# A two-layer diffusion backbone: the feed-forward network's own work is scheduled ahead of the adaLN vectors and state-space tables made beside it

## The chip, the cores and the metric

The kernel runs on one core of one Trainium2 chip. The time is that of one execution on the device, in microseconds (us), and the median of several executions is compared. TensorE (PE in the profile, with PEld for its weight loads) multiplies matrices, VectorE (DVE), ScalarE (ACT) and GpSimd (POOL) work elementwise, SyncE (SP) issues nearly all DMAs.

## What is computed

Two trunk layers of a backbone over 640 tokens (128 of context, 512 latent) of width 1024:

```python
for l in range(DEPTH):                                   # DEPTH = 2
    mod = silu(c) @ w_ada[l] + b_ada[l]                  # adaLN: shifts, scales, gates
    h   = layer_norm(x) * (1 + scale1) + shift1
    z   = h @ w_in[l]                                    # one combined projection
    mix = concat(ssm(z), neighbourhood_attention(z), gqa(z))
    x   = layer_norm(ALPHA * x + gate1 * (mix @ w_out[l]), g1, b1)
    h   = layer_norm(x) * (1 + scale2) + shift2
    u   = silu(gate(h)) * up(h)                          # SwiGLU: w_ffn_in, 2 x 2816 columns
    x   = layer_norm(ALPHA * x + gate2 * (u @ w_ffn_out[l]), g2, b2)
```

The state-space group (ssm) needs tables of powers of the discretised poles, which depend on the weights of its layer alone. All is float32.

## The kernel before

The 640 tokens are five tiles of 128. A float32 matrix product is three products of halves: each operand is split in a high and a low part (`split`, L283 a cast on ACT, L284 a subtraction on POOL or DVE), and `mm3` (L309 to L313) multiplies high by high, low by high and high by low. Tiles `wh`, `wl` hold split weights (from raw `wr`), `hh`, `hl` the split normalised input, `xs` the split output of the network's first half.

The feed-forward network, `ffn` (L1725), runs over 22 blocks f of 128 hidden columns, in six parts (`PARTS`, 4, 4, 4, 3, 4, 3). A block is made by `ffn_in` (L1624): weights loaded, combined and split (`ffn_in_weights`, L1597 the combinations on DVE), seven products of half-size blocks on PE, their sums on DVE (L1647), two Silu on ACT (L1651 to L1660), the gating (L1663, L1665 on DVE) and the split into `xs` (L283, L284). The first `EARLY` = 2 blocks are made by `ffn_in_plain` without the combinations, a generator of two halves. After each part the part's blocks, collected in `gT`, are multiplied with their rows of `w_ffn_out` (`product`, ten to a part: two halves of 512 columns by five tiles): the gate on DVE (L1764) and the running sum on DVE (L1766, L1771; in the last part `residual`, L1303, which sums rows as well). The last part stands in its own branch (L1773 to L1802): per tile two products into PSUM banks `psS` (two buffers of two banks), then the post-LayerNorm (`post_ln`: L1288 and L1298 on DVE, L257 on ACT, the power -1/2 at L230 on POOL), the next layer's normalisation (L273 on ACT), its transposition (L417 on PE), modulation (L423 on DVE, L425 on ACT), the split into `hh` and `hl`, and the first products with the next layer's `w_in`.

Beside this network the kernel makes what the next layer needs, as `ffn_side` (L1822): two generators, of which each block with f >= `SIDE0` = 2 takes one step. One is adaLN (`ada_side`, 12 half vectors: loads into `ev`, matmuls L381, transpositions L386 and L398). The other is `ssm_tables` (in layer 0 only): after its powers, four groups h of a table B (`powtab`: per group four products L615 and two sums L617 on DVE, then matmuls L631 and L635, transpositions L655, copies L639 and L658, two small operations L642 and L644, stores L646, L648 and L659) and four groups of a table C (L615, L617 and the stores L664). Both work in the four buffers `ev`, which the next layer's weight pieces (`begin`, halves split into `ev` and `ys`) use too. What is left of the side work is asked for at the start of the last part, ahead of its products in the program.

The order of the instructions on each engine is made when the program is built: a scheduler takes, of what is ready by its own count, the instruction that stands first in the program. `tc.high_priority(n)` makes what is written inside it stand n instructions earlier for that choice; `PRIO` is 300 (L1459). Before the change it wraps the preparation and the units of neighbourhood attention only. `tc.issue_after(ins)` holds the side step until the instruction `ins` (here the gating of the block) has been placed.

```python
            for f in range(f0, f0 + nf):
                gT.append(next(plain[f]) if f < self.EARLY else self.ffn_in(l, f, H))
                if f >= self.SIDE0:
                    with self.tc.issue_after(self.mark.ins):
                        next(side, None)
```

Of the kernel before, what the change touches and what calls it, by code (L numbers as in the profile page):

```python
# [157 lines left out]
class Build:  # L158
# [1566 lines left out]
    def ffn(self, l, xs, M, H, nxt, ada):  # L1725
        nc, I = self.nc, self.I
        V, S = nc.vector, nc.scalar
        side = self.ffn_side(l, nxt, ada)
        rows = {}

        def row(key, src):
            if key not in rows:
                rows[key] = self.bcast_row(src)
            return rows[key]

        wo = I["w_ffn_out"][l].rearrange("(k p) n -> p k n", p=128)
        f0 = 0
        for key, cd in (("gp", 0), ("gs", 1)):
            row(key, M["gates"][1, cd])
        for part, nf in enumerate(PARTS):  # L1740
            gT = []
            plain = [self.ffn_in_plain(l, f, H) for f in range(f0, min(f0 + nf, self.EARLY))]
            for p in plain:
                next(p)
            for f in range(f0, f0 + nf):
                gT.append(next(plain[f]) if f < self.EARLY else self.ffn_in(l, f, H))
                if f >= self.SIDE0:
                    with self.tc.issue_after(self.mark.ins):
                        next(side, None)
            last = part == len(PARTS) - 1  # L1750

            def weights(n):
                cs = slice(n * 512, (n + 1) * 512)
                return [b for k0 in range(0, nf, 2) for b in self.wload(wo[:, f0 + k0:f0 + min(k0 + 2, nf), cs])]

            def product(n, i, w, ps=None, sums=None):
                cs = slice(n * 512, (n + 1) * 512)
                ps = ps or self.psA()
                for k in range(nf):
                    a = self.cols(i)  # L1760
                    self.mm3(ps, a(gT[k][0]), a(gT[k][1]), *w[k], k == 0, k == nf - 1)
                g = row("gp", M["gates"][1, 0]) if i == 0 else row("gs", M["gates"][1, 1])
                t = ps
                V.tensor_tensor(out=t, in0=ps, in1=g[:, cs], op=ALU.mult)  # L1764
                if part == 0:
                    V.scalar_tensor_tensor(out=xs[i][:, cs], in0=xs[i][:, cs], scalar=ALPHA, in1=t, op0=ALU.mult,  # L1766
                                           op1=ALU.add)
                elif last:
                    self.residual(xs[i][:, cs], t, sums[n])
                else:  # L1770
                    V.tensor_tensor(out=xs[i][:, cs], in0=xs[i][:, cs], in1=t, op=ALU.add)  # L1771

            if last:  # L1773
                if l + 1 < L:
                    self.function(AF.Exp, self.after)
                w = [weights(n) for n in range(2)]
                junk = self.k4(),
                for _ in side:
                    pass
                if l + 1 < L:  # L1780
                    A = nxt["A"] = self.begin(l + 1, nxt["M"], True)
                for m, i in enumerate(self.ORD):
                    if l + 1 < L:
                        two = self.psS()
                        two = two[:, 0], two[:, 1]
                    else:
                        two = [self.psA() if b else self.psS()[:, 0] for b in self.LB[m]]
                    sums = self.columns("fsum")
                    for n in range(2):
                        product(n, i, w[n], two[n], sums)  # L1790
                    out = self.xout[l][i]
                    parts = self.halves(out) if m == NT - 1 and l == L - 1 else None
                    s = self.post_ln(xs[i], row("lg", I["ln2_g"][l]), row("lb", I["ln2_b"][l]), sums, junk,
                                     self.LNF[l][m], parts)
                    if not parts:
                        nc.sync.dma_start(out, xs[i])
                    if l + 1 < L:
                        self.normalise(xs[i], self.halves(xs[i]), self.stats_of(xs[i], s, junk, "lsn"),
                                       self.NORMV[1])
                        for j in self.ORD[max(m - 1, 0):m] + self.ORD[m:] * (m == NT - 1):  # L1800
                            A["tile_in"](j, xs[j])
                            A["tile_pieces"](j)  # L1802
            else:
                for n in range(2):
                    w = weights(n)
                    for i in self.ORD:
                        product(n, i, w)
            f0 += nf

    def ada_side(self, l, M, nxt):  # L1810
# [104 lines left out]
```

## Time and profile before

| | |
|---|---|
| runs | 1800.53 us median of 3 (1794.71 to 1801.53) |
| profiled execution | 1788.01 us, its span 1786.0 us, mean granted clock 0.960 |
| PE busy | 1641.2 us, 92% of the span, 11624 matmuls |
| DVE busy | 1222.5 us, 68% |
| ACT, POOL busy | 827.3 us (46%), 763.5 us (43%) |
| network of layer 0, its parts | 478 to 941 us, PE busy 444.20 of 463 us |
| network of layer 1, its parts | 1337 to 1758 us, PE busy 411.76 of 421 us |
| layer 0's end and layer 1's first products | 941 to 1003 us, PE busy 49.9 of 62 us |

The span runs from the first to the last instruction of the profiled execution. A busy PE is not a PE at its peak, since the clock that it is granted varies; a stretch in which it is idle or granted less is time that other work could give back. Times in a timeline are microseconds from the start of the span.

### The profile page before, as it was taken

To read this page: it belongs to the slowest core of one execution; us is meant where nothing else is said; L and a number is where in the kernel's file an instruction comes from. 1 tells how busy PE (TensorE), PEld (TensorE's weight loads), DVE (VectorE), ACT (ScalarE), POOL (GpSimd) and SP (SyncE) were. 2 spreads that over 40 slices of the span, in tenths; PEclk is the share of its full clock that TensorE was granted. 3 is DMA by queue.
4 is the path that set the end of the run, shared out by engine and by line. 5 is a ranking of instruction groups with operands and counts; after the bars stand their busy time and mean duration, and the time that the engine had idled before them with its cause. 6 is when DMAs were issued, how large, how long until landed. Compare 5 with 4: busy or idle time off the path is not lost. (4 is left out here: it accounts for less than half of the span.)

```text
span 1786.0 us, 31489 instructions
## 1 busy us (share of the span) xinstructions
PE 1641.2 (92%) x11624; PEld 1435.8 (80%) x11624; DVE 1222.5 (68%) x2460; ACT 827.3 (46%) x1800; POOL 763.5 (43%) x651
## 2 busy tenths in 40 slices
PE   5899899898899999999897989998979999999997
PEld 2898677676788888798796978876859899998995
DVE  5765546627678776778877565565487687876777
ACT  5444446657443334243345556665574242433433
POOL 3853203059235343346266232111785254454463
PEclk9999899798999999999999999998989999999999
DMA  9445767446353645232324243463542231222212
GB/s 335 112 126 139 238 194 213 123 158 203 107 172 122 195 127 182 81 121 71 121 85 157 92 129 96 111 187 115 180 148 85 94 107 59 92 74 69 98 62 81
DMA packets 183114, 234.90 MB, mean 132 GB/s; under 512 B 78960, under 2 KB 112048, under 8 KB 182960
## 3 DMA queue, kind: packets, MB, share of 16 engines
q1 hardware_dynamic: 182960, 232.88, 42.3%
q8 instruction: 92, 1.51, 0.3%
q14 instruction: 62, 0.51, 0.1%
HBM read 203.57 MB, written 29.39 MB: 130 GB/s over the span
## 5 line engine op out<-in xcount | busy, mean ns | idle before, releaser
L284 POOL TENSOR_TENSOR wl<-wr,wh 128x512 fp32r<-128x512 f32 x362 | 504.2, 1413 | 522.8 <-ACT wh L283 343.2
L283 ACT CAST wh<-wr 128x512 fp32r<-128x512 f32 x450 | 275.2, 619 | 383.9 <-DVE wr L1597 88.6
L311 PE MATMUL psM<-hh,wh 128*128 128x320 f32 x560 | 180.3, 322 | 2.3 <-DVE ys L1647 1.1
L313 PE MATMUL psM<-hh,wl 128*128 128x320 f32 x560 | 177.9, 318 | 0.0
L312 PE MATMUL psM<-hl,wh 128*128 128x320 f32 x560 | 177.8, 318 | 0.0
L311 PEld LDWEIGHTS psM<-hh,wh 128*128 128x128 f32 x560 | 108.5, 194 | 6.2 <-issue 1.8
L311 PE MATMUL psT<-hh,wh 128*128 128x320 f32 x352 | 109.9, 312 | 0.0
L313 PEld LDWEIGHTS psM<-hh,wl 128*128 128x128 f32 x560 | 108.6, 194 | 1.5 <-issue 1.4
L312 PE MATMUL psT<-hl,wh 128*128 128x320 f32 x352 | 109.2, 310 | 0.0
L313 PE MATMUL psT<-hh,wl 128*128 128x320 f32 x352 | 109.0, 310 | 0.0
L312 PEld LDWEIGHTS psM<-hl,wh 128*128 128x128 f32 x560 | 108.7, 194 | 0.3
L230 POOL TENSOR_TENSOR sm<-sm,mhalf 128x1 f32<-128x1 f32 (+2 forms) x46 | 54.3, 1182 | 92.3 <-DVE sm L260 49.3
L1647 DVE TENSOR_TENSOR ys<-ys,psM 128x320 f32<-128x320 f32 x140 | 65.0, 481 | 33.8 <-PE psM L313 31.9
L1160 DVE TENSOR_REDUCE psS<-psS 128x1 f32<-128x640 f32 x64 | 52.7, 828 | 47.4 <-PE psS L1157 45.6
L1647 DVE TENSOR_TENSOR ys<-ys,psT 128x320 f32<-128x320 f32 x140 | 65.0, 481 | 28.8 <-PE psT L313 27.7
L311 PE MATMUL psT<-b,wh 128*128 128x320 f32 x240 | 76.5, 319 | 8.3 <-DVE ys L1647 7.4
L311 PE MATMUL psM<-b,wh 128*128 128x320 f32 x240 | 76.1, 317 | 5.8 <-DVE ys L1647 5.8
L284 POOL TENSOR_TENSOR wl<-ws,wh 128x512 fp32r<-128x512 f32 x40 | 53.6, 1340 | 64.4 <-ACT wh L283 62.6
L859 PE MATMUL psT<-ident,ys 128*128 128x128 f32 x440 | 73.2, 285 | 5.8 <-DVE hl L284 3.3
L311 PE MATMUL psM<-wh,xs 128*128 128x512 f32 x190 | 74.9, 394 | 3.7 <-DVE k L1771 3.5
L311 PE MATMUL psT<-wh,xs 128*128 128x512 f32 x190 | 75.6, 398 | 2.9 <-DVE k L1771 2.9
L1597 DVE TENSOR_TENSOR ws<-wr,wr 128x512 f32<-128x512 f32 x40 | 37.0, 926 | 58.9 <-DMA wr<-in_w_ffn_in_dram 28.3
(440 smaller groups left out, 4907.9 us busy)
## 6 DMA issues: line engine op xcount, KB each, us to landing
wr<-in_w_ffn_in_dram SPq DMA_DIRECT2D x88, 512.0 KB, 3.7
ev<-in_w_ada_dram SPq DMA_DIRECT2D x112, 256.0 KB, 4.0
wr<-in_w_ffn_out_dram SPq DMA_DIRECT2D x40, 512.0 KB, 3.9
wr<-in_w_out_dram SPq DMA_DIRECT2D x32, 512.0 KB, 3.6
wr<-in_w_in_dram SPq DMA_DIRECT2D x28, 512.0 KB, 4.8
wa<-in_w_ada_dram SPq DMA_DIRECT2D x24, 512.0 KB, 4.7
k<-in_x_dram SPq DMA_DIRECT2D x10, 512.0 KB, 5.6
xs<-zqk SPq DMA_DIRECT2D x32, 160.0 KB, 3.7
```

The costliest lines, as they stand in the source:

```text
L230: self.nc.gpsimd.tensor_tensor(out=o, in0=v, in1=self.mhalf.broadcast_to([128, v.shape[1]]), op=ALU.pow)
L283: nc.scalar.copy(hi, src)
L284: (lo_eng or nc.vector).tensor_tensor(out=lo, in0=src, in1=hi.bitcast(F32), op=ALU.subtract)
L311: nc.tensor.matmul(ps, lhsT=ah, rhs=bh, start=first, stop=False)
L312: nc.tensor.matmul(ps, lhsT=ah, rhs=bl, start=False, stop=False)
L313: nc.tensor.matmul(ps, lhsT=al, rhs=bh, start=False, stop=last)
L859: self.nc.tensor.transpose(pt[:, j * 128:(j + 1) * 128], s, self.ident)
L1160: V.tensor_reduce(out=m, in_=sp[:, :, 0:320], axis=AX.XY, op=ALU.max, negate=True)
L1597: V.tensor_tensor(out=o, in0=x, in1=y, op=op)
L1647: V.tensor_tensor(out=o, in0=x, in1=y, op=ALU.add)
```

## The change

The blocks f of the network (for f below `EARLY`, their second half) and the products of every part but the last are written inside `high_priority(PRIO)`, in both layers. The side steps, the first halves of the plain blocks and the whole last part are not. No instruction is added or taken away.

```diff
             for f in range(f0, f0 + nf):
-                gT.append(next(plain[f]) if f < self.EARLY else self.ffn_in(l, f, H))
+                with self.tc.high_priority(self.PRIO):
+                    gT.append(next(plain[f]) if f < self.EARLY else self.ffn_in(l, f, H))
                 if f >= self.SIDE0:
                     with self.tc.issue_after(self.mark.ins):
                         next(side, None)
...
             else:
-                for n in range(2):
-                    w = weights(n)
-                    for i in self.ORD:
-                        product(n, i, w)
+                with self.tc.high_priority(self.PRIO):
+                    for n in range(2):
+                        w = weights(n)
+                        for i in self.ORD:
+                            product(n, i, w)
             f0 += nf
```

Behind the first line of the diff the numbers of lines grow by one (L1764 becomes L1765), behind the second by two.

The order of DVE in part 4 of layer 0's network before the change: table C (`ev_9409` to `ev_9415` is its group 1) among the sums and gatings of two blocks.

```order
L1647 TENSOR_TENSOR ys_9300<-ys_9300,psM_9389 128x320
L1665 TENSOR_TENSOR ys_9300<-ys_9300,ys_9301 128x320
L615 TENSOR_TENSOR ev_9409<-k_1346_7183,k_1345_7180 128x512
L615 TENSOR_TENSOR ev_9410<-k_1346_7183,k_1345_7180 128x512
L615 TENSOR_TENSOR ev_9414<-k_1346_7183,k_1345_7180 128x512
L615 TENSOR_TENSOR ev_9415<-k_1346_7183,k_1345_7180 128x512
L1647 TENSOR_TENSOR ys_9301<-ys_9301,psT_9374 128x320
L617 TENSOR_TENSOR ev_9409<-ev_9409,ev_9410 128x512
L617 TENSOR_TENSOR ev_9414<-ev_9414,ev_9415 128x512
L1663 TENSOR_TENSOR ys_9300<-ys_9300,ys_9301 128x320
```

After the change no operation of table C stands in any part of the network on DVE.

The order of DVE at the end of layer 0's network before the change, from the last block's gating (L1665) on: `psS_10467` and `psS_10512` are the products of the last part's first two tiles, `k_888` is the first tile's residual.

```order
L1665 TENSOR_TENSOR ys_10266<-ys_10266,ys_10267 128x320
L284 TENSOR_TENSOR xs_10265<-ys_10266,xs_10264 128x320 x2
L1764 TENSOR_TENSOR psS_10467<-psS_10467,k_982_5298 128x512
L1764 TENSOR_TENSOR psS_10512<-psS_10512,k_982_5298 128x512
L1303 SCALAR_TENSOR_TENSOR k_888_4838,sm_10468<-k_888_4838,psS_10467 128x512
L1303 SCALAR_TENSOR_TENSOR k_886_4835,sm_10513<-k_886_4835,psS_10512 128x512
L1764 TENSOR_TENSOR psS_10467<-psS_10467,k_982_5298 128x512
L1303 SCALAR_TENSOR_TENSOR k_888_4838,sm_10468<-k_888_4838,psS_10467 128x512
L252 TENSOR_SCALAR sm_10495<-sm_10468 128x1
L1764 TENSOR_TENSOR psS_10512<-psS_10512,k_982_5298 128x512
L1303 SCALAR_TENSOR_TENSOR k_886_4835,sm_10513<-k_886_4835,psS_10512 128x512
L260 TENSOR_SCALAR sm_10495<-sm_10495 128x1
```

The next row is the first tile's L1288. The same place after the change begins so:

```order
L1665 TENSOR_TENSOR ys_10266<-ys_10266,ys_10267 128x320
L615 TENSOR_TENSOR ev_8758<-k_1346_7183 128x512
L615 TENSOR_TENSOR ev_8759<-k_1346_7183 128x512
L284 TENSOR_TENSOR xs_10265<-ys_10266,xs_10264 128x320 x2
L617 TENSOR_TENSOR ev_8758<-ev_8758,ev_8759 128x512
L615 TENSOR_TENSOR ev_8763<-k_1346_7183 128x512
L615 TENSOR_TENSOR ev_8764<-k_1346_7183 128x512
L642 TENSOR_TENSOR ev_8929<-eye_146,dcol_5859 16x64
L617 TENSOR_TENSOR ev_8763<-ev_8763,ev_8764 128x512
L1765 TENSOR_TENSOR psS_10467<-psS_10467,k_982_5298 128x512
```

and 42 rows further, with the rest of the 20 L615 and 10 L617 of B's last group and of all of C between, comes to the first tile's LayerNorm:

```order
L1765 TENSOR_TENSOR psS_10754<-psS_10754,k_982_5298 128x512
L615 TENSOR_TENSOR ev_9735<-k_1346_7183,k_1345_7180 128x512
L1303 SCALAR_TENSOR_TENSOR k_806_4440,sm_10755<-k_806_4440,psS_10754 128x512
L617 TENSOR_TENSOR ev_9734<-ev_9734,ev_9735 128x512
L252 TENSOR_SCALAR sm_10778<-sm_10755 128x1
L1765 TENSOR_TENSOR psS_10875<-psS_10875,k_982_5298 128x512
L260 TENSOR_SCALAR sm_10495<-sm_10495 128x1
L1288 SCALAR_TENSOR_TENSOR k_888_4838<-k_888_4838,sm_10495,k_1975_10491 128x1024
L1303 SCALAR_TENSOR_TENSOR k_804_4437,sm_10876<-k_804_4437,psS_10875 128x512
L1298 SCALAR_TENSOR_TENSOR k_888_4838,sm_10501<-k_888_4838,sm_10495,k_1976_10493 128x1024
```

The first L1288 stood behind two tiles' products and now stands behind all ten L1765 and the tables.

On POOL, in the same place, the two powers (L230) of the first tile's statistics stood one behind the other before the change:

```order
L284 TENSOR_TENSOR wl_11157<-wr_11154,wh_11156 128x512
L230 TENSOR_TENSOR sm_10495<-sm_10495,mhalf 128x1
L230 TENSOR_TENSOR sm_10504<-sm_10504,mhalf 128x1
L230 TENSOR_TENSOR sm_10536<-sm_10536,mhalf 128x1
L284 TENSOR_TENSOR wl_11161<-wr_11154,wh_11160 128x512
```

and after it they stand among the splits of the next layer's weights:

```order
L284 TENSOR_TENSOR ys_10421<-wr_10423,ev_10417 128x256
L230 TENSOR_TENSOR sm_10495<-sm_10495,mhalf 128x1
L284 TENSOR_TENSOR ys_10421<-wr_10433,ev_10418 128x256 x2
L284 TENSOR_TENSOR ys_10422<-wr_10433,ev_10419 128x256 x2
L284 TENSOR_TENSOR wl_11287<-wr_11284,wh_11286 128x512
L1010 TENSOR_TENSOR ys_11081<-ys_11081,zt_11082 128x640
L284 TENSOR_TENSOR wl_11291<-wr_11284,wh_11290 128x512
L230 TENSOR_TENSOR sm_10504<-sm_10504,mhalf 128x1
```

The casts into `ev_10416` to `ev_10419`, which those splits read, need `ev` buffers that tables still hold, and `wr_11284` is loaded behind table C's last store on SP.

## Rows read from the trace of the kernel before

**Rows 1.** The page: busy time, share and instructions; one costliest group.

```profile
PE 1641.2 (92%) x11624; PEld 1435.8 (80%) x11624; DVE 1222.5 (68%) x2460; ACT 827.3 (46%) x1800; POOL 763.5 (43%) x651
...
L284 POOL TENSOR_TENSOR wl<-wr,wh 128x512 fp32r<-128x512 f32 x362 | 504.2, 1413 | 522.8 <-ACT wh L283 343.2
```

**Rows 2.** Busy time by stretch: both networks, then layer 0's end in two.

```profile
core 0: us, PE busy (x) PEld busy (x) DVE busy (x) ACT busy (x) POOL busy (x), PEclk, DMA share, GB/s
478.00:941.00 463.00, 444.20 (x3050) 396.02 (x3049) 353.78 (x643) 167.06 (x331) 195.40 (x142) 0.99 0.40 124
1337.00:1758.00 421.00, 411.76 (x2427) 383.78 (x2428) 319.40 (x486) 159.27 (x307) 197.56 (x145) 0.99 0.25 81
941.00:973.00 32.00, 24.56 (x102) 18.75 (x101) 25.19 (x60) 18.45 (x38) 23.11 (x26) 0.95 0.46 149
973.00:1003.00 30.00, 25.37 (x195) 24.24 (x195) 24.24 (x56) 22.55 (x45) 10.76 (x9) 0.94 0.35 124
```

**Rows 3.** What PE waited for, 800 to 880 us.

```profile
engine line waited for: us in total, times, longest us
PE psM L311 <- DVE ys L1647: 3.7, 3, 2.6
PE psT L311 <- DVE ys L1647: 2.9, 1, 2.9
```

**Rows 4.** Busy time by stretch, as rows 2, of 10 us each.

```profile
830.00:840.00 10.00, 7.37 (x44) 7.11 (x43) 9.84 (x17) 3.12 (x7) 3.61 (x3) 0.89 0.28 96
840.00:850.00 10.00, 10.00 (x66) 10.00 (x65) 9.74 (x9) 3.40 (x7) 8.06 (x6) 0.94 0.16 53
850.00:860.00 10.00, 7.06 (x38) 6.80 (x37) 9.60 (x16) 4.22 (x9) 6.16 (x5) 0.83 0.37 107
```

**Rows 5.** Groups of instructions, 478 to 941 us: busy, mean ns | idle before.

```profile
L615 DVE TENSOR_TENSOR ev<-k,k 128x512 f32<-128x512 f32 x16 | 18.8, 1231 | 0.0
...
L615 DVE TENSOR_TENSOR ev<-k 128x512 f32<-128x512 f32 x16 | 13.6, 882 | 0.0
...
L617 DVE TENSOR_TENSOR ev<-ev,ev 128x512 f32<-128x512 f32 x16 | 11.7, 743 | 0.0
...
L631 PE MATMUL psS<-k,ev 128*128 128x32 f32 x64 | 9.2, 275 | 0.0
...
L655 PE MATMUL psS<-ident,ev 128*128 128x128 f32 x32 | 4.8, 272 | 0.0
```

**Rows 6.** Timeline of DVE: start, duration, engine, line.

```profile
841.71 6.90 DVE L615 TENSOR_TENSOR ev<-k,k 128x512 f32<-128x512 f32 x4
...
873.87 2.49 DVE L615 TENSOR_TENSOR ev<-k,k 128x512 f32<-128x512 f32 x4
...
877.28 0.68 DVE L617 TENSOR_TENSOR ev<-ev,ev 128x512 f32<-128x512 f32 x1
```

**Rows 7.** Busy time by stretch, as rows 2.

```profile
870.00:880.00 10.00, 10.00 (x54) 8.85 (x53) 9.90 (x20) 3.57 (x7) 0.00 (x0) 1.00 0.73 239
```

**Rows 8.** Timeline of DVE at layer 0's end.

```profile
944.87 1.74 DVE L284 TENSOR_TENSOR xs<-ys,xs 128x320 fp32r<-128x320 f32 x2 [0.83 <-ACT xs L283]
946.53 1.28 DVE L1764 TENSOR_TENSOR psS<-psS,k 128x512 f32<-128x512 f32 x2
947.73 0.67 DVE L1303 SCALAR_TENSOR_TENSOR k<-k,psS 128x512 f32<-128x512 f32 x1
...
954.29 1.64 DVE L1288 SCALAR_TENSOR_TENSOR k<-k,sm,k 128x1024 f32<-128x1024 f32 x1
...
957.62 1.28 DVE L1298 SCALAR_TENSOR_TENSOR k<-k,sm,k 128x1024 f32<-128x1024 f32 x1 [0.96 <-POOL sm L230]
```

**Rows 9.** Timeline of ACT at layer 0's end.

```profile
960.29 1.15 ACT L257 ACTIVATE k<-k,sm 128x1024 f32<-128x1024 f32 x1 [6.50 <-DVE sm L254]
...
963.73 1.52 ACT L273 ACTIVATE k<-k,sm 128x512 f32<-128x512 f32 x2 [0.92 <-DVE sm L267]
```

**Rows 10.** Timeline of PE at layer 0's end.

```profile
944.89 0.50 PE L311 MATMUL psS<-wh,xs 128*128 128x512 f32 x1 [0.98 <-ACT xs L283]
...
959.58 0.50 PE L311 MATMUL psS<-wh,xs 128*128 128x512 f32 x1 [2.66 <-DVE k L1303]
...
972.74 0.39 PE L311 MATMUL psM<-ev,hh 128*128 128x256 f32 x1 [0.16 <-ACT hh L283]
```

## The prediction

> **What bounds the kernel now.** I began with the page: PE is busy 92% of the span and DVE 68% [rows 1], so a time that PE loses for want of operands is lost to the end, and DVE has room only on average. Then I read busy time by stretch [rows 2]. In the network of layer 0, which carries the tables, PE is idle 18.8 of 463 us (4.1%); in that of layer 1, which carries none, 9.2 of 421 us (2.2%). The reader is to see there what the change can win at most in layer 0 and that little is left to win in layer 1. At layer 0's end, 941 to 1003 us, PE is idle 12.1 of 62 us and DVE 12.6 us: a place where neither engine has much to spare and where, as the order shows, the displaced work arrives.
>
> Next, PE's waits between 800 and 880 us, where table C is made [rows 3]: 6.6 us, all for one line of DVE, the sums of the network's products (L1647), in four waits of which two are over 2.5 us. The stretches of 10 us there [rows 4] show DVE busy 9.6 to 9.8 of 10 and a granted clock of 0.89, 0.94 and 0.83 in a network whose mean is 0.99 [rows 2]. So DVE is the bound in that place: four L615 in a row take 6.90 us at 841.71 [rows 6], and the sum that PE waits for stands behind them.
>
> **What the change does, by the order.** No instruction comes or goes. In layer 0's network DVE's sums and SP's weight loads move ahead of side work, and the last group of table B and all of table C (20 L615, 10 L617) leave the network altogether. They reappear on DVE between the last block's gating and the first LayerNorm of layer 0's end, woven with the products' gates and sums. Layer 1 has only two side steps left; I cost its small reorderings at nothing, because PE's idle time there is already low [rows 2].
>
> **What layer 0's network gains.**
> - The waits of rows 3 go: 6.6 us. What PE is late for next is the DMA or another sum, which I leave as it is.
> - Clock: 10 us at 0.89, 0.94 and 0.83 cost 1.1, 0.6 and 1.7 us against a granted clock of 1.0, together 3.4 us [rows 4]. If PE does not stop there, I expect them back.
> - PE's work for the moved tables leaves the stretch: one of four groups of L631 and L655, (9.2 + 4.8) / 4 = 3.5 us [rows 5], and another group's L655, 1.2 us, which now stands behind the last block's products, where PE waits anyway: 4.7 us.
>
> Sum 14.7 us. The lower bound is the 4.7 us alone, if other side work takes the place of the waits; the upper is all idle time, 18.8 us, with 4.7 and about 4.6 us of clock (1% of 463 us): 28 us. I take 14.7, since these are waits with a name and the 12 us of other idle time have none that the change removes.
>
> **What layer 0's end loses.** Before, from the split of the last block (944.87) to the first L1288 (954.29) DVE takes 9.4 us, and the first product with layer 1's weights starts at 972.74 [rows 8, 10], 27.9 us behind the split. Behind it in the program the LayerNorms of the other tiles follow, DVE busy 24.24 of 30 us [rows 2].
>
> After, DVE has before its first L1288: the split 1.7 us, ten gates at 0.64, nine L1303 at 0.67 [rows 8], and about 2 us of small operations (estimate): 16 us. To this come the tables. Cheap end: L615 at 2.49 / 4 = 0.62 and L617 at 0.68 [rows 6], 20 x 0.62 + 10 x 0.68 = 19.2 us. Dear end: the means of the network, 4 x 0.88 + 16 x 1.23 + 10 x 0.74 = 30.6 us [rows 5]. I take 25, between them: POOL is busy 23.11 of 32 us at this place [rows 2], which speaks for the dear end, but its splits there now wait for buffers that the tables hold. So L1288 starts about 41 us behind the split (35 to 47).
>
> From L1288 to the first product the shortest chain is 1.27 to 1.64 for L1288, 1.28 for L1298 with the power before it, two L257 of which one counts, 1.15, 1.52 for L273 [rows 8, 9], then transposition, modulation and cast, some 3 us (estimate), and a power and small operations, 1 to 2 us: 9 to 11 us. Before it took 18.4 us, because products stood between, but these ran beside it. Now the power on POOL stands behind two weight splits of 1.4 us each [rows 1] and an addition, and Squares on ACT stand behind casts whose buffers and loads wait for the last table: I add 2 to 4 us and take 13. The first product starts 41 + 13 = 54 us behind the split instead of 27.9: 26 us later. PE's ten products end meanwhile and hide nothing of it; the moved table matmuls fit in. Behind the first product nothing is given back: the four other tiles' LayerNorms still need DVE, and before, two of them had already begun. I put 1 us on the granted clock falling while PE waits, as it does at this place already, 0.94 to 0.95 [rows 2]. Loss 27 us, bounds 18 (cheap tables, shortest chain) and 36.
>
> **The sum.** 1788.0 - 14.7 + 27 = 1800.3, that is 12 us or 0.7% slower than the profiled execution's own time. That execution lies 12.5 us below the median of the three runs, 1800.53; on the median I forecast **1812.5 us**.
>
> **A rule weighed against the rows.** Four L615 with two different inputs took 6.90 us where POOL was busy 8.06 of 10 us, and 2.49 us where it did nothing [rows 4, 6, 7]: 1.73 against 0.62 us each. The Trainium skill (SBUF — State Buffer, "SBUF: two separate sides") says that VectorE and GpSimd share a pair of ports as an exclusive lock, and that an operation with two SBUF inputs against a GpSimd operation reading SBUF blocks fully until the other ends. The rows agree in direction. By the rule at its strictest the tables' 19.2 us and POOL's 23.11 us could not overlap at all at layer 0's end: 42 us in place of 25, and the whole change 29 us slower. The sum stays with 25, because in the network POOL's share of 42% [rows 2] gives means of 0.88 to 1.23 us and not the full block.
>
> **Rivals.**
> - *The tables fit into DVE's gaps (the side not slower).* At layer 0's end DVE is idle 12.6 of 62 us [rows 2]. If the tables run at the cheap price and DVE has no pause left in this stretch, its end moves only by 19.2 - 12.6 = 6.6 us. With the network of layer 0 at layer 1's idle share, 8.7 us fewer instead of 6.6, the gain is 16.8 and the result 10 us faster, 1790. For it: in the new order DVE has something ready at nearly all times. Against it: the first L1288 is behind all of it, so that PE sits idle 20 us with nothing to do and the later tiles need DVE as much as before. It decides from the point where the first product comes less than about 42 us behind the split.
> - *Cheap end and short chain.* Loss 18 instead of 27, gain 14.7: 3 us slower, 1804, no change that can be told.
> - *Dear end.* Tables at the network's price or under the port rule, powers and Squares stuck behind loads: loss 36, 21 us slower, 1822; with the gain at its lower bound, 4.7 us, against the forecast loss, the same.
> - *The change does nothing for the network.* The order says otherwise, and I give it almost nothing.
>
> **Chances and range.** About 0.5%, 9 us, is what a measurement of this kernel can tell from no change. The forecast, 10 to 18 us slower, has 0.38; the dear end 0.17; the cheap end and what lies around it, within 9 us either way, 0.30; tables in the gaps, faster by more, 0.15. So faster 0.15, same 0.30, slower 0.55. The range from 1791 to 1829 takes in the cheap end, the near edge of the gaps and most of the dear end; the forecast's own range is 1809 to 1819.
>
> **What would show it.** In the profile after: the waits of rows 3 are gone and the granted clock of the parts where table C stood is at 0.99 or above; PE's idle time in layer 0's network is some 10 us. In the stretch after the last block's split stand 20 L615 and 10 L617, 19 to 31 us of DVE, the first L1288 starts 35 to 47 us behind the split, and the first product with layer 1's weights 45 to 62 us behind it, with PE idle most of the 20 us before. Layer 1's network takes what it took. I am wrong if the first product comes within 42 us of the split, if the network of layer 0 shortens by over 25 us or not at all, or if PE's new waits in it are for side work's loads or for DVE as before.

## The result and the profile after

The change makes the kernel slower: 1884.44 us (median, 1881.96 to 1887.8) against 1797.62 us before, a ratio of 1.0496 with the 95% interval [1.0469, 1.0523]. That is 87 us; I had forecast 12.

The page of the profile after, its engines and the row of granted clocks:

```profile
PE 1682.9 (90%) x11624; PEld 1455.1 (77%) x11624; DVE 1204.1 (64%) x2460; ACT 823.7 (44%) x1798; POOL 760.9 (40%) x651
...
PEclk9999998897999999999986999999989999899999
```

Against [rows 1] DVE is not busier but less busy (1204.1 for 1222.5 us), and PE is busy 41.7 us longer with the same 11624 matmuls. To see where, I cut each execution at events that both kernels have. The two fences give first and last start of lines: the transpositions just ahead of each network (L417 on `ys`; the first start stands ahead of network 0, the last ahead of network 1), the first gate into `psS` (L1764, now L1765, layer 0's end begins), the last transposition behind it (L417 on `k`) and the last sum of the second network (L1647). Before:

```profile
L417 PE MATMUL psT<-ident,k x80: 270/273/476, 17.9 to 1002.1; 128*128 128x128 f32 x80
L417 PE MATMUL psT<-ident,ys x32: 271/273/421, 449.0 to 1336.2; 128*128 128x128 f32 x32
...
L1764 DVE TENSOR_TENSOR psS<-psS,k x20: 682/696/700, 946.5 to 1775.7; 128x512 f32<-128x512 f32 x20
...
L1647 DVE TENSOR_TENSOR ys<-ys,psT x140: 468/480/490, 498.2 to 1752.1; 128x320 f32<-128x320 f32 x140
```

After:

```profile
L417 PE MATMUL psT<-ident,k x80: 270/300/476, 17.8 to 1064.4; 128*128 128x128 f32 x80
L417 PE MATMUL psT<-ident,ys x32: 272/273/421, 448.0 to 1398.2; 128*128 128x128 f32 x32
...
L1765 DVE TENSOR_TENSOR psS<-psS,k x20: 680/694/700, 974.6 to 1870.1; 128x512 f32<-128x512 f32 x20
...
L1647 DVE TENSOR_TENSOR ys<-ys,psT x140: 468/481/490, 504.9 to 1847.0; 128x320 f32<-128x320 f32 x140
```

Differences of these starts, in us, for all kernels of this study, each from one profiled execution (the last column is from the row of L381, adaLN's matmuls, in layer 0's network; "groups" counts how often the program's order of PE changes to them there):

| kernel | network 0 | its end | layer 1 up to its network | network 1 | span | groups; L381 busy |
|---|---|---|---|---|---|---|
| before | 497.5 | 55.6 | 334.1 | 415.9 | 1786.0 | 43; 26.8 |
| after | 526.6 | 89.8 | 333.8 | 448.8 | 1880.1 | 90; 44.1 |
| zero | 543.8 | 52.8 | 341.4 | 449.3 | 1874.9 | 68; 33.4 |
| only1 | 502.5 | 57.2 | 335.5 | 452.8 | 1837.2 | 43; 27.2 |
| onlyf | 513.3 | 56.0 | 336.5 | 436.2 | 1833.5 | 50; 30.3 |
| onlyp | 512.5 | 56.5 | 338.8 | 425.6 | 1825.8 | 50; 29.5 |
| ord300 | 538.5 | 55.3 | 338.0 | 414.3 | 1831.3 | 118; 51.5 |
| ord1200 | 511.7 | 80.3 | 338.6 | 414.4 | 1837.4 | 94; 43.7 |
| oa300 | 498.7 | 57.1 | 343.6 | 411.1 | 1798.8 | 37; 25.9 |
| oa600 | 498.6 | 52.1 | 332.2 | 411.7 | 1786.4 | 40; 27.1 |
| oa900 | 503.5 | 52.1 | 341.7 | 414.5 | 1799.9 | 40; 26.3 |
| oa1200 | 490.5 | 81.4 | 337.6 | 408.7 | 1804.8 | 39; 26.4 |
| aftada | 528.2 | 55.4 | 343.9 | 445.7 | 1861.8 | 61; 31.5 |

How far such a segment can be trusted is seen from only1, whose order is that of before up to layer 1's network: its first network starts 6.8 us later and takes 5.0 us more. Differences below some 5 us in one segment mean nothing.

The loss has three parts of like size: network 0 +29.1, its end +34.2, network 1 +32.9. The forecast had -14.7, +27 and 0. The second part has the right sign but is too small; the first has the wrong sign and the third was not foreseen at all, though layer 1 makes no tables. The prediction cuts at the last block's split, not at the first gate. The gate now stands 7.1 us behind that split instead of 1.7, so cut at the split the end costs 39.7 us and network 0 23.6.

What PE waits for in network 1 after (1399 to 1848 us):

```profile
PE psM L311 <- DVE ys L1647: 8.1, 4, 3.1
PE psT L311 <- DVE ys L1647: 7.6, 6, 2.4
PE psM L311 <- DVE k L1772: 7.5, 3, 2.5
PE psT L311 <- DVE k L1772: 2.9, 2, 1.7
PE psS L311 <- ACT ys L1703: 2.8, 1, 2.8
```

and before (1337 to 1753 us):

```profile
PE psT L311 <- DVE k L1771: 2.5, 1, 2.5
PE psT L311 <- DVE ys L1647: 2.4, 4, 0.8
PE psM L311 <- DVE ys L1647: 1.6, 2, 1.1
```

Waits for the network's own sums have grown from 4.0 to 15.7 us (L1647) and from 2.5 to 10.4 (L1771, now L1772), where almost no side work stands in DVE's way. Busy time by stretch says the same: PE busy 418.58 of 449 us at a granted clock of 0.97, where [rows 2] has 411.76 of 421 at 0.99.

```profile
1399.00:1848.00 449.00, 418.58 (x2406) 387.45 (x2406) 305.52 (x476) 157.19 (x303) 196.26 (x143) 0.97 0.24 75
```

So the order among the network's own pieces had got worse. What the program does there can be read while it is built: `high_priority` takes 300 from the running number that it gives to instructions, and on leaving puts the number back to what it was on entering. It does not go on by the length of what stood inside. In layer 1 each of the 20 blocks behind the plain ones begins at 6202 and ends at 6322, and the products of each of the first five parts begin at 6202 as well: the scheduler has no way to prefer an older block, and the first instructions of a new block stand ahead of the last ones of an older one. In layer 0 the side steps push the number on, but only by their own length (0 to 101; a block takes 120): from the first block behind the plain ones to the last, blocks begin at 2913, 3014, 3101 and so on to 3631. There they overlap, and the last block begins ahead of every side step made from block 8 on (3636 and higher), so that a boost of 300 which rewinds leads by more than half of the network. The order of PE in layer 1's network after the change, where before each of these products ran through in one or two pieces (the last product of one block, `psM_15181`, among three products of the next):

```
psM_15181 x2, psT_15166 x12, psT_15242 x2, psM_15181 x4, psT_15242 x10, psM_15255 x12,
psT_15269 x2, psM_15181 x5, psT_15269 x10, psM_15181 x1, psT_15299 x12
```

### The profile page after: what moved, and what is told of

The parts are those of the page before. It is cut to its first block, busy times and chain, and to the rows that moved or that the text cites. A ratio compares the mean times of both kernels' runs of the same rounds, so it can differ in the third digit from the quotient of the medians.

```text
span 1880.1 us, 31371 instructions
## 1 busy us (share of the span) xinstructions
PE 1682.9 (90%) x11624; PEld 1455.1 (77%) x11624; DVE 1204.1 (64%) x2460; ACT 823.7 (44%) x1798; POOL 760.9 (40%) x651
## 4 chain that ended last, share of the span: by engine, by line
PE 64%; DVE 12%; DMA 10%; POOL 6%; issue 4%; ACT 3%; SPq 1%; POOLq 0%; DVEq 0%; ACTq 0%
PE psM L311 9%; PE psM L312 9%; PE psM L313 8%; PE psT L311 6%; PE psT L312 5%; PE psT L313 5%; DMA wr<-in_w_ffn_in_dram 3%; POOL wl L284 3%; PE psT L859 3%; PE psS L311 2%; PE psS L1157 2%; PE psS L312 2%; DVE wr L1597 2%; PE psS L313 2%; PE psT L1184 2%
## 5 line engine op out<-in xcount | busy, mean ns | idle before, releaser
L284 POOL TENSOR_TENSOR wl<-wr,wh 128x512 fp32r<-128x512 f32 x362 | 500.2, 1399 | 589.3 <-ACT wh L283 458.4
L1647 DVE TENSOR_TENSOR ys<-ys,psM 128x320 f32<-128x320 f32 x140 | 64.5, 481 | 81.9 <-PE psM L313 80.5
L230 POOL TENSOR_TENSOR sm<-sm,mhalf 128x1 f32<-128x1 f32 (+2 forms) x46 | 54.7, 1191 | 99.0 <-DVE sm L260 52.0
L1647 DVE TENSOR_TENSOR ys<-ys,psT 128x320 f32<-128x320 f32 x140 | 65.0, 481 | 45.4 <-PE psT L313 44.1
L311 PE MATMUL psM<-wh,xs 128*128 128x512 f32 x190 | 78.3, 412 | 7.5 <-DVE k L1772 7.5
L313 PE MATMUL psM<-wh,xs 128*128 128x512 f32 x190 | 76.7, 404 | 0.0
```

Of the source, the lines that this page charges most:

```text
L230: self.nc.gpsimd.tensor_tensor(out=o, in0=v, in1=self.mhalf.broadcast_to([128, v.shape[1]]), op=ALU.pow)
L284: (lo_eng or nc.vector).tensor_tensor(out=lo, in0=src, in1=hi.bitcast(F32), op=ALU.subtract)
L311: nc.tensor.matmul(ps, lhsT=ah, rhs=bh, start=first, stop=False)
L313: nc.tensor.matmul(ps, lhsT=al, rhs=bh, start=False, stop=last)
L1647: V.tensor_tensor(out=o, in0=x, in1=y, op=ALU.add)
```

## The experiments

Theory T: these ties cost the networks their time, in both layers. Rival L: the lead over the side work costs it. A third theory, S, came from what ord300 showed.

**ord300.** Both `with` lines of the change call this instead:

```diff
-                with self.tc.high_priority(self.PRIO):
+                with self.ahead():
...
+    LEAD = 300
+    def ahead(self):                      # a context manager
+        with self.tc.high_priority(self.LEAD):
+            p = self.tc.cur_priority
+            yield
+            n = self.tc.cur_priority - p
+        self.tc.cur_priority += n
```

> The same boost of 300 as the change, but behind each boosted piece the program's counter goes on by the piece's length, so that blocks and products keep their order among themselves. Theory T (ties: the counter comes back to its old value behind each boosted piece, so that all blocks of a network start at one priority and are mixed): near before, 1797 within 10 us, layer 1's network at 416 us, tables inside layer 0's network. Rival L (the lead over side work is itself what costs): near the change, 1875 to 1890.

Measured: 1833.78 us, 1.0196 [1.0161, 1.0232]. Neither. Network 1 is back at 414.3 us, as T says; but network 0 takes 538.5, more than with the change. Something else in layer 0 costs 40 us, and it is neither ties nor late tables (its end takes 55.3). The tables are not late because here the number goes on: the last block begins at 6785, behind all the side steps.

**zero.** Ties without a lead:

```diff
-                with self.tc.high_priority(self.PRIO):
+                with self.tc.high_priority(0):
```

> The change with a boost of 0 in place of 300: pieces have no lead over side work, but the counter still comes back behind each. Tables end in the network as before. T: layer 1's network 30 us longer than before and layer 0's 20 to 37 us longer, layer 0's end as before: 1847 to 1866. L: as before, 1797 within 10 us.

Measured: 1879.63 us, 1.0449 [1.0414, 1.0484], all but the whole loss without any lead. Network 1 takes 449.3 us, +33.4; network 0 +46.3, 9 us more than I had allowed. So network 1 has its whole loss without any lead, and L falls there. It does not fall for layer 0's end, which is as before here, 52.8 us: the change's 34 us there do come from the lead. That the totals are so near is chance, since zero loses 17 us more in network 0 and nothing at the end. Nor is zero ties alone in layer 0: a side step begins at the number at which its block began, not behind the block, so side work has moved forward as well.

**ord1200.** As ord300 with `LEAD = 1200`.

> Order among the pieces kept as in ord300, but a lead of 1200: by the order the rest of the tables stands at layer 0's end, as in the change, ahead of the first LayerNorm. T: layer 1's network as before (416 us), layer 0's network up to 15 us shorter, the first product with layer 1's weights 60 us and more behind the last split instead of 27.9: 1810 to 1830. L: 1875 or more.

Measured: 1831.66 us, 1.018 [1.0136, 1.0225], just above the range. Network 1 at 414.4; the end 80.3, 25 us longer; network 0 511.7, not shorter but 14 us longer: again the unknown cost of ord300, a part of it.

**only1.**

```diff
-                with self.tc.high_priority(self.PRIO):
+                with self.tc.high_priority(self.PRIO) if l == 1 else nullcontext():
```

> The change in layer 1 alone, where no tables are made and only two adaLN steps are left. T: layer 1's network 449 us instead of 416, all else as before: 1825 to 1835. A rival by which layer 1's loss is only an after-effect of layer 0's order (buffers, clock): 1797 within 5 us.

Measured: 1834.15 us, 1.0195 [1.0158, 1.0232]; network 1 takes 452.8 us. Layer 1's loss is its own.

**What ord300 pays for.** Its network 0 shows hardly more recorded waits than the others, and PE "busy" without a gap from 600 to 720 us. The groups of L381 in that network, before, after and in ord300:

```profile
L381 PE MATMUL psS<-ev,silc 128*32 128x128 f32 x576 | 26.8, 282 | 3.6 <-DMA ev<-in_w_ada_dram 3.3
```

```profile
L381 PE MATMUL psS<-ev,silc 128*32 128x128 f32 x576 | 44.1, 285 | 7.4 <-DMA ev<-in_w_ada_dram 7.2
```

```profile
L381 PE MATMUL psS<-ev,silc 128*32 128x128 f32 x576 | 51.5, 283 | 0.0
```

The same 576 records (two to each of 288 matmuls) of the same mean length, yet nearly twice the busy time: they overlap each other where they stand together, and not where they stand alone. The timeline of PE, before:

```profile
590.52 0.31 PE L311 MATMUL psM<-b,wh 128*128 128x320 f32 x1
590.66 0.31 PE L312 MATMUL psM<-b,wh 128*128 128x320 f32 x1
590.90 0.65 PE L381 MATMUL psS<-ev,silc 128*32 128x128 f32 x16
591.48 0.41 PE L313 MATMUL psM<-b,wl 128*128 128x320 f32 x1
591.82 0.64 PE L381 MATMUL psS<-ev,silc 128*32 128x128 f32 x16
```

and in ord300:

```profile
600.11 0.41 PE L381 MATMUL psS<-ev,silc 128*32 128x128 f32 x2
600.45 0.41 PE L312 MATMUL psM<-b,wh 128*128 128x320 f32 x1
600.79 0.41 PE L381 MATMUL psS<-ev,silc 128*32 128x128 f32 x2
601.12 0.41 PE L313 MATMUL psM<-b,wl 128*128 128x320 f32 x1
```

Network matmuls in a row start 0.14 us apart (590.52, 590.66). From one L381 to the next in ord300 it is 0.68 us for two records and one network matmul; before, 0.92 us (590.90 to 591.82) for 16 records and one network matmul. So a record costs (0.92 - 0.68) / 14 = 0.017 us and each visit to L381 some 0.68 - 0.14 - 0.03 = 0.5 us, however few it brings. All visits that stand between network matmuls without idle time say much the same: from the network matmul before to the one behind, the median is 0.68 us for 2 records (74 visits in ord300) and, before the change, 0.67 for 8 (20 visits), 0.81 for 16 (5) and 1.25 for 32 (3). A further record costs nothing measurable up to 8 and 0.02 to 0.03 us beyond. The granted clock was 1.00 from 600 to 640 us, so it is not the clock. L381 uses a quarter of PE's columns (128*32), the network all (128*128). The Trainium skill (TensorEngine Tiling (Array Packing), "Key Properties") says that changing the tiling mode drains TensorE, without a price; the timeline fits that and puts the price at 0.5 us there and back. Whether it is the drain or the weight load that then can't be hidden is not told apart here.

ord300 visits L381 118 times, before 43: 75 visits more at 0.5 us are 38 us. Its network 0 is 41 us longer, and PE is busy 507.26 us in it instead of 470.10, 37 us more. This is theory S.

**oa300.** As ord300, with the adaLN steps in the same lead, so that only the tables lag:

```diff
-            a, b = next(ada, 0), next(tab, 0)
+            with self.ahead():
+                a = next(ada, 0)
+            b = next(tab, 0)
```

> As ord300 (lead of 300, pieces keep their order), but the adaLN steps have the same lead, so that only the tables lag: by the order the adaLN matmuls (L381) in the network then stand in 37 groups instead of 118 (before the change 43). Theory S (ord300's loss is adaLN matmuls put one by one between the network's, each a change of shape that PE pays for): L381's busy time in layer 0's network falls from 51.5 us to 25 to 30, and the time is 1797 within 12 us. Rival (the lead over the tables is the loss): it stays at 1820 to 1840.

Measured: 1800.55 us, 1.0015 [0.9994, 1.0036]. Network 0 falls from 538.5 to 498.7 us with 37 visits; 81 fewer at 0.5 us are 40. S holds, and with ties and single visits gone the lead of 300 over the tables costs nothing and brings nothing.

**oa1200.** As oa300 with `LEAD = 1200`.

> As oa300 with a lead of 1200: most of the rest of the tables stands at layer 0's end ahead of the first LayerNorm, with no ties and whole groups of adaLN matmuls (39). This is the loss that I had forecast, alone. S, with my forecast's gain in the network of 10 to 15 us: L381 25 to 30 us, layer 0's end 20 to 27 us longer than before, 1803 to 1815. If late tables cost as much as the change's end shows (34 us): 1815 to 1825.

Measured: 1808.19 us, 1.0066 [1.0043, 1.0089]: inside the range of S. Against ord1200, with the same lead, 55 visits fewer (27 us at 0.5) make network 0 21.2 us shorter. Here is most of what I had forecast, 16 of the 20 L615 and 8 of the 10 L617 behind the last split, without ties and with the visits as they were: network 0 7 us shorter, its end 25.8 us longer, together 0.7% slower. What PE waits for at that end (960 to 1036 us):

```profile
PE psT L417 <- ACT k L273: 13.4, 1, 13.4
PE psS L311 <- DVE k L1303: 4.7, 3, 3.7
```

**onlyf** and **onlyp.** One of the change's two `with` lines each.

```diff
# onlyf: the products without the boost; onlyp: the blocks without it
-                with self.tc.high_priority(self.PRIO):
+                with nullcontext():
```

> The change without its second part: only the blocks are boosted, the products are not. T: blocks tie among themselves in both layers, which I hold for most of the loss: layer 1's network 440 to 450 us, total 1850 to 1880. Rival (it is products that tie with the next part's blocks): layer 1's network 416 to 425 us, total below 1835.

> The change's second part alone: only the products are boosted. T: products of one part come in order by themselves, layer 1's network 416 to 425 us, total 1795 to 1820. Rival: layer 1's network 435 us or more, total 1830 or more.

Measured: onlyf 1836.81 us, 1.0221 [1.018, 1.0263], network 1 436.2, both below what T had said and above the rival's; onlyp 1821.42 us, 1.0117 [1.0082, 1.0151], network 1 425.6, and the total slightly above its range. Blocks that tie among themselves cost network 1 20 us, products that come early 10 us, both together 33. I had put too much on the blocks: both parts of the change do harm. In network 0 each alone costs 15 to 16 us.

**oa600, oa900.** As oa300 with these leads.

> As oa300 with a lead of 600: ties gone, adaLN matmuls in 40 groups, all tables still inside layer 0's network, later than in oa300. Theory: the network of layer 0 near oa1200's 490 us and layer 0's end near before's 56 us, so 1785 to 1797, perhaps the first version faster than before. Rival (the gain of oa1200's network is that its tables are not in it): as oa300, 1795 to 1803.

> As oa600 with a lead of 900, one operation of the tables left behind the last block's gating. Theory: 1785 to 1800; rival: tables pile up in the last blocks, network of layer 0 500 us or more, 1800 to 1810.

Measured: oa600 1787.85 us (12 runs), 0.9945 [0.9918, 0.9972]; oa900 1801.52 us, 1.0014 [0.9991, 1.0036]. oa600 is the one version that is faster than both kernels, by 0.3 to 0.8%. My reason for it fell: its network 0 takes 498.6 us, no less than before and 8 more than oa1200's. Its gain is spread over segments by less than they vary between executions (end 52.1, network 1 411.7), so where it comes from stays open. oa900's network 0 takes 503.5 us, and its time lies in the rival's range. What is left for oa1200's shorter network is the rival's reading, work that left it; its 7 us are little more than such a segment varies.

**aftada.** The change, with its own (restoring) boost for the adaLN steps too:

```diff
-            a, b = next(ada, 0), next(tab, 0)
+            with self.tc.high_priority(self.PRIO):
+                a = next(ada, 0)
+            b = next(tab, 0)
```

> The change itself (ties left as they are) with the same boost for the adaLN steps: by the order their matmuls stand in 61 groups instead of 90 (before 43), and no table operation is left behind the last block's gating. T with S: both networks keep the ties' 33 us, L381 takes some 33 us, layer 0's end is as before, 53 to 57 us: 1850 to 1870. If ties were not the main cause: below 1830.

Measured: 1856.76 us, 1.0323 [1.0273, 1.0374], inside the range. Network 1 445.7 us, network 0 528.2: both keep the ties; the end is back at 55.4, since by the order the tables get their turn inside the network.

## Why the prediction was wrong

**Layer 0's end: the right mechanism, too small.** I had 20 L615 and 10 L617 ahead of the first LayerNorm, 25 us of DVE. The groups between 966 and 1012 us after:

```profile
L615 DVE TENSOR_TENSOR ev<-k,k 128x512 f32<-128x512 f32 x16 | 11.1, 712 | 3.4 <-ACT wh L283 3.1 <-DMA tabC<-ev 0.3
L617 DVE TENSOR_TENSOR ev<-ev,ev 128x512 f32<-128x512 f32 x10 | 7.8, 777 | 0.0
L615 DVE TENSOR_TENSOR ev<-k 128x512 f32<-128x512 f32 x4 | 3.5, 925 | 1.2 <-DMA tabV<-ev 1.2
```

22.4 us busy and 4.6 us of waiting for buffers and stores ahead of them. The split is at 967.48 and the first L1288 at 1011.02, 43.5 us behind it (forecast 41, range 35 to 47); the last line is the stretch between them, its columns as in [rows 2]:

```profile
967.48 0.49 DVE L284 TENSOR_TENSOR xs<-ys,xs 128x320 fp32r<-128x320 f32 x1
...
979.85 0.45 DVE L644 TENSOR_TENSOR ev<-ev 16x64 f32<-16x64 f32 x1 [3.85 <-ACT ev L639]
...
1011.02 1.32 DVE L1288 SCALAR_TENSOR_TENSOR k<-k,sm,k 128x1024 f32<-128x1024 f32 x1
...
967.48:1011.02 43.54, 32.16 (x122) 23.27 (x122) 34.11 (x67) 9.46 (x24) 12.86 (x12) 0.82 0.44 139
```

That 43.5 is so near to 41 is partly luck: DVE was busy 34.1 us where I had added up 41 of work, and idle 9.4 us, for which I had no term (for 3.85 of them L644, a small operation of the tables, waited for ACT).

The chain behind it was the mis-sized term: 13 us forecast, 19.9 measured, 18.4 before. It did not shorten as I had said. The timeline of POOL at that place:

```profile
1019.16 1.26 POOL L284 TENSOR_TENSOR wl<-wr,wh 128x512 fp32r<-128x512 f32 x1
1020.39 1.52 POOL L1010 TENSOR_TENSOR ys<-ys,zt 128x640 f32<-128x640 f32 x1
1021.88 2.24 POOL L284 TENSOR_TENSOR wl<-wr,wh 128x512 fp32r<-128x512 f32 x1
1024.08 0.54 POOL L230 TENSOR_TENSOR sm<-sm,mhalf 128x1 f32<-128x1 f32 x1
```

The power that the chain needs (L230) stands behind exactly the two splits and the addition that I named, 5 us of them, against the 2 to 4 that I had added for all queues. L1298 before it had also waited 2.56 us for the first power, which stood behind four splits. PE:

```profile
1026.77 1.97 PE L417 MATMUL psT<-ident,k 128*128 128x128 f32 x8 [16.46 <-ACT k L273]
1030.92 0.58 PE L311 MATMUL psM<-ev,hh 128*128 128x256 f32 x1 [2.18 <-ACT hh L283]
```

It waited 16.46 us in one piece, and the first product came 63.4 us behind the split, where [rows 8, 10] have 27.9 and I had 54 (45 to 62). From there to the last transposition it took 33.5 us instead of 29.4, at a mean granted clock of 0.87 instead of 0.94, where I had put 1 us on the clock. From the split on, the loss is 39.7 us against a forecast of 27 and an upper bound of 36. In oa1200 it is 26.7, but there too two errors cancel: the first L1288 stands 34.8 us behind the split, with fewer tables, and the chain takes 19.8.

On the rule weighed in the prediction: the two-input L615 took 0.71 us each here, near the 0.62 of the quiet row and far from the 1.73 beside a busy POOL. But POOL was busy only 12.86 of the 43.5 us in which the tables ran, 30%, where I had reckoned with 23.11 of 32, so this place does not test the rule at its strictest.

**Network 0: wrong sign.** The step that failed is the sum of 14.7 us built on "In layer 0's network DVE's sums and SP's weight loads move ahead of side work". It had no term for the adaLN matmuls, which I had counted as work that moves at no price. The sums did move ahead: PE's waits for L1647 in this network fell from 10.2 us (the first two lines) to 4.9:

```profile
PE psM L311 <- DVE ys L1647: 5.2, 5, 2.6
PE psT L311 <- DVE ys L1647: 5.0, 2, 2.9
...
PE psT L311 <- DVE ys L1647: 3.0, 4, 1.2
PE psM L311 <- DVE ys L1647: 1.9, 3, 0.7
```

But the order before me had the adaLN matmuls one by one between the network's, in 90 visits instead of 43, and L381's busy time rose from 26.8 to 44.1 us. Network 0 before, after and in zero:

```profile
449.00:946.50 497.50, 470.10 (x3242) 417.21 (x3240) 379.80 (x690) 185.99 (x369) 208.51 (x154) 0.98 0.41 127
...
448.00:974.60 526.60, 493.58 (x3207) 422.04 (x3205) 351.82 (x666) 184.10 (x361) 203.08 (x151) 0.96 0.37 113
...
454.60:998.40 543.80, 493.76 (x3243) 428.63 (x3241) 372.82 (x691) 186.08 (x369) 207.19 (x155) 0.96 0.38 117
```

PE is busy 23.5 us longer, about what 47 visits cost at 0.5 us (the table matmuls that left and the lower granted clock work against each other in that sum), and idle 33.0 us instead of 27.4. The sum also took the boost for a shift of 300 that leaves the network's own order alone. zero shows what a disturbed order can cost network 0: 46.3 us, of which 25 visits make 12; its waits for L1647 are 20.3 us and PE's idle time is 50.0. In the change itself little of that is seen. As for the gain, oa1200, where neither cost is present, has 7 us, about half of what I took.

**Network 1: not foreseen.** The step is "I cost its small reorderings at nothing, because PE's idle time there is already low". Low idle time meant that there was nothing to win; it said nothing of what a worse order could lose. The difference was in the order of PE in plain sight, in some 950 lines of difference for 2500 rows. It cost 33 us, shown by only1 and zero with it and by ord300, ord1200 and oa300 without.

The rivals turned on the tables or on the size of the gain; none had the network harming itself. The sum of the three parts, 29 + 34 + 33 = 96 us, is close to the difference of the spans (94.1 us).

What stays open: the price of the lost order in network 0 was not measured by itself, for no run has the change with its visits at 43. PE's idle time there is 50.0 us in zero and 44.1 in aftada, but 33.0 in the change. DVE's load is a possible reason, not tested: in network 0 it is busy 372.82 and 373.08 us in those two, which make all the tables there, and 351.82 in the change.

## What to carry to other kernels

A scheduler's priority is a number, and before using a helper that rewinds it one should look at what the number is behind the helper: here every boosted block of layer 1 restarted at one value, and the lost order among 20 like blocks cost 33 us in that network of 416. When side work is demoted, ask of each kind what becomes of it: work of another shape on PE must stay in groups, and work with a due date must still be done before it (oa600 keeps order and groups, lets only the tables lag, and stops before they reach the layer's end). And a stretch with little idle time has little to win from a new order and can still lose by it, so its price is not zero.

## What the runs showed of the hardware

Each visit of PE to matmuls on 32 of its columns among matmuls on all 128 cost 0.5 us, at a granted clock of 1.00, beside 0.14 us from one network matmul to the next. What it brought mattered little: 0.68 us from network matmul to network matmul for 2 records of L381, 0.67 for 8, 0.81 for 16. It appears as busy time, not as waiting: in ord300 PE is "busy" without a gap from 600 to 720 us, visits included, and only the busy time of the one group, or the distance of starts in the timeline, gives it away.
